# A hybrid encoder layer on one core: the projection's weights loaded at once into the filters' memory, and Hyena's projection begun at the last quarter of the sequence

## The chip, the cores and the metric

The kernel runs on one core of one Trainium2 chip. The metric is the time of one execution on the device in microseconds (us), the median of several runs. The core's engines are named as the profile names them: PE multiplies matrices (PEld loads the stationary operand for it), DVE, ACT and POOL work on vectors, SP issues most of the DMAs. Each engine takes its instructions in the order in which the program has them and waits at each one until what it needs is there. A "granted clock" of 1.00 in the profile is PE's full clock.

## The reference

One layer over 2048 tokens of width 1024, all float32. Cut to what the change touches:

```python
a = rms_norm(h, norm1_g)
proj = a @ w_in                               # (2048, 1024) @ (1024, 2304)
q, k, v, u = split(proj, [512, 640, 768])     # attention's columns, then Hyena's 1536
...                                           # per-head norm and rotary positions of q and k
att = block_attention(q, k, v)                # 8 query heads, 2 key heads of 64
uc = short_conv(u, conv_w, conv_b)            # three taps along the sequence, then the long filters
z = concatenate([t, cos(ang), -sin(ang)])     # the filters' own small network
h = sin(freq * (z @ w1 + b1)); h = sin(freq * (h @ w2 + b2)); h = sin(freq * (h @ w3 + b3))
...                                           # filters applied by Fourier transforms, output projection, MLP
```

## The kernel before

Matrix products of float32 are made of three products of rounded parts: each operand is split into a high part and the rest (`mm3`, lines 168 to 170: high by high, high by rest, rest by high). The norm's gain goes into the weights: ACT writes `wh` = weight times gain, rounded, and DVE writes `wl`, the rest (`split_w`, lines 214 and 215).

The program runs in stages. The first is `qkv_proj` together with pieces of two other generators, which it advances a step at a time with `pump`: `side` is `filter_hidden`, the hidden layers of the long filters, and `u` is `u_proj`, Hyena's projection and short convolution. In this stage the order of instructions on PE, DVE, ACT and POOL is the order of the code (`in_order`); SP's order is chosen by the scheduler. The second stage is `attention`, in which the scheduler mixes the rest of `u_proj` and the filters' taps into the attention steps. After it come the Fourier transforms of the filters and of Hyena's convolutions, the output projection and the MLP, which the change doesn't touch.

`qkv_proj` goes over 16 tiles of 128 tokens, in a pipeline that a loop over `i` writes out by hand. A tile of x is loaded (`xt`), squared and scaled by its norm (`xs`, lines 225 and 231), transposed on PE (`tp`, line 240), split into the high part `ah` (ACT, line 243) and the rest `al` (DVE, line 249), and multiplied with the weights: 8 by 3 matmuls of 512 columns for q and as many of 256 columns for k and v (`qkv`). Then ACT takes the result (`y`, `z`, line 272 on), DVE norms and rotates it (`rotation`), PE transposes it again (`tq`, line 316), and it is stored to DRAM (`q_d`, `k_d`, `v_d`). Both parts of every transposed tile are stored too, in `aT_d`, for `u_proj`.

The weights come in 16 pieces, eight of 128x512 for q and eight of 128x256 for k and v (`wraw`, line 210), into three buffers of the one and four of the other. SP issues a load when its buffer is free, that is when ACT and DVE have split the piece before it.

`filter_hidden` has its own memory (`f1`). Its first step, at `i` = 1, issues 16 small DMAs from POOL's queue and has DVE scale the loaded `fr` (line 1329); each of the next two steps issues a load of `z` (line 1345, POOL's queue again) and right behind it the matmuls `fo` that read it (line 1339). Later steps are matmuls, three DVE instructions each, sines on ACT, and copies into `hc`.

`u_proj` multiplies in 4 blocks of 512 tokens, from the first to the last, with 12 column tiles each, so 48 units of 8 times three matmuls (`uo`). A block's operand is loaded back from `aT_d` in eight pieces (`aT`, line 423). In the first block each unit's weights are loaded raw (`uraw`, line 434), split by ACT and DVE (`uw`, lines 438 and 440) and stored in `uw_d`, from where the other blocks load them; weights and raw weights have two buffers each, and the load for unit n+1 is issued when unit n begins. The result is copied (`u`), convolved by one ACT and two DVE instructions (`uy`) and stored. Within a block a unit is 10 steps of the generator. Before attention 38 steps of units are taken (the last 30 by `START`): not quite four units.

Of the kernel before, what the change touches and what calls it, by code (L numbers as in the profile page):

```python
# [172 lines left out]
def small_tables(k):  # L173
# [9 lines left out]
    nc.vector.tensor_scalar_mul(out=k.qkg[:, 0], in0=k.qkg[:, 0], scalar1=HD ** -0.5)  # L183


def qkv_proj(k, pa, ps, side, u):

    nc, a = k.nc, k.a
    x, w_in = a["x"][0], a["w_in"][0]
    root = pa.tile([P, 1], F32, name="root", bufs=1)  # L190
# [15 lines left out]
    raws = {}  # L206

    def load_w(d, c0, c1):
        raws[d, c0] = pw.tile([P, c1 - c0], F32, name=f"wraw{c0}", bufs=4 if c0 else 3)
        nc.sync.dma_start(out=raws[d, c0][:], in_=w_in[d * P:(d + 1) * P, c0:c1])  # L210

    def split_w(d, c0, c1):
        raw = raws.pop((d, c0))
        nc.scalar.mul(out=wh[:, d, c0:c1], in_=raw[:], mul=k.g1[:, d:d + 1])
        nc.vector.scalar_tensor_tensor(out=wl[:, d, c0:c1], in0=raw[:], scalar=k.g1[:, d:d + 1],
                                       in1=f32(wh[:, d, c0:c1]), op0=ALU.mult, op1=ALU.subtract)

    def load_x(t):
        xt[t] = pw.tile([P, DM], F32, name="xt", bufs=3)
        nc.sync.dma_start(out=xt[t][:], in_=x[t * P:(t + 1) * P, :])  # L220

    def squared(t):
        xs[t] = pa.tile([P, DM], F32, name="xs", bufs=3)
        ssq = pa.tile([P, 1], F32, name="ssq")
        nc.scalar.activation(out=xs[t][:], in_=xt[t][:], func=AF.Square, accum_out=ssq[:])
        rs[t] = []
        return rstd_steps(k, pa, ssq[:], DM, 1, "rstd", rs[t])

    def scaled(t):
        r, = rs.pop(t)  # L230
        nc.scalar.mul(out=xs[t][:], in_=xt.pop(t)[:], mul=r[:])
# [14 lines left out]
    def turned_low(t):  # L246
# [3 lines left out]
        for i, part in enumerate((hi, lo)):  # L250
            nc.sync.dma_start(out=k.aT_d[i, :, t * P:(t + 1) * P].rearrange("(d p) t -> p d t", p=P), in_=f32(part[:]))
# [79 lines left out]
    for d in range(4):  # L331
        load_w(d, *q_cols)
    load_x(1)
    for d in range(4, ND):
        load_w(d, *q_cols)
    for d in range(4):
        load_w(d, *kv_cols)
    load_x(2)
    for d in range(4, ND):
        load_w(d, *kv_cols)  # L340
    nc.gpsimd.dma_start(out=qkg[:, 0], in_=a["q_norm_g"].to_broadcast([P, HD]))
    nc.gpsimd.dma_start(out=qkg[:, 1], in_=a["k_norm_g"].to_broadcast([P, HD]))
    k.qkg = qkg
    small_tables(k)
    ahead = {-2: range(4), -1: range(4, ND)}
    for i in range(-3, NT + 2):
        norms = rot = iter(())
        own, mine = 0 <= i < NT, 0 <= i - 2 < NT
        tail = i >= NT
        if 2 < i + 5 < NT:  # L350
            load_x(i + 5)
# [4 lines left out]
        if tail:  # L356
            pump(u, 2)
# [9 lines left out]
        if 0 <= i + 2 < NT:  # L367
            scaled(i + 2)
        if i == -2:
            turned(0)  # L370
            turned_low(0)
        for d in ahead.get(i, ()):
            split_w(d, *q_cols)
        pump(rot)
        if 0 <= i + 3 < NT:
# [6 lines left out]
        if tail:  # L382
            pump(u, 2)
# [3 lines left out]
        if 0 < i + 1 < NT:  # L387
            turned(i + 1)
        pump(rot)
        if 0 < i + 1 < NT:  # L390
            turned_low(i + 1)
        if i == 0:
            for d in range(ND):
                split_w(d, *kv_cols)
# [9 lines left out]
        if i > 0:  # L404
            pump(side)
        pump(u, {NT - 5: 1, NT - 4: 3, NT - 3: 3, NT - 2: 3}.get(i, 0))
        if i == NT - 1:
            pw_pool.__exit__(None, None, None)
            pump(u)
# [4 lines left out]
def u_proj(k):  # L414
    nc, a = k.nc, k.a
    w_in = a["w_in"][0]
    nct = 3 * HYW // P
    H, NB = 512, 4
    cw, cb = k.cw, k.cb

    def load_a(b, d):
        t = pu.tile([P, 2, H], F32R, name="aT", bufs=ND)
        nc.sync.dma_start(out=f32(t[:]), in_=k.aT_d[:, d * P:(d + 1) * P, b * H:(b + 1) * H].rearrange("a p t -> p a t"))
        return t

    def load_w(b, ct):

        w = uws[(b * nct + ct) % 2]
        if b:
            nc.sync.dma_start(out=f32(w[:]), in_=k.uw_d[ct])  # L430
            return w, iter(())
        c0 = 768 + ct * P
        raw = raws[ct % 2]
        nc.sync.dma_start(out=raw[:], in_=w_in[:, c0:c0 + P].rearrange("(d p) c -> p d c", p=P))

        def split():
            for d in range(ND):
                nc.scalar.mul(out=w[:, 0, d], in_=raw[:, d], mul=k.g1[:, d:d + 1])  # L438
                if d in UW_VEC:
                    nc.vector.scalar_tensor_tensor(out=w[:, 1, d], in0=raw[:, d], scalar=k.g1[:, d:d + 1],  # L440
                                                   in1=f32(w[:, 0, d]), op0=ALU.mult, op1=ALU.subtract)
                else:
                    nc.gpsimd.tensor_mul(out=raw[:, d], in0=raw[:, d], in1=k.g1[:, d:d + 1].to_broadcast([P, P]))
                    nc.gpsimd.tensor_sub(out=w[:, 1, d], in0=raw[:, d], in1=f32(w[:, 0, d]))
                yield
            nc.sync.dma_start(out=k.uw_d[ct], in_=f32(w[:]))
            yield

        return w, split()

    uws, raws = [k.uf.tile([P, 2, ND, P], F32R, name="uw0")], [k.uf.tile([P, ND, P], F32, name="uraw0")]
    nw, rest = load_w(0, 0)
    yield
    for _ in rest:
# [3 lines left out]
    aT = [load_a(0, d) for d in range(ND)]  # L458
    uws.append(pu.tile([P, 2, ND, P], F32R, name="uw1", bufs=1))
# [1451 lines left out]
```

## Time and profile before

| | |
|---|---|
| median of 3 runs | 3138.62 us (3138.4 to 3143.3) |
| profiled execution | 3142.1 us, of which the span of instructions is 3140.3 us |
| mean granted clock of PE | 0.977 |
| PE busy | 2976.8 us, 95% of the span |
| DVE, ACT, POOL busy | 1984.8, 1394.4, 1713.8 us |
| moved by DMA | 534.16 MB, 170 GB/s over the span |

The profile is one execution, about 3.5 us above the median. A row of a timeline has the start, the duration, engine, line and operation, output and inputs, and in brackets the idle time of that engine just before and what ended it. A row of windows has the busy time and the count of instructions of each engine in a stretch, then the granted clock, the busy share of the DMA engines and GB/s. A row of a group has the count, then busy time and the mean of one in ns, then the idle time before them and its causes.

### The profile page before, as it was taken

Reading aid. Unit: us, or ns where it says so; the run is one execution under the profiler, and the core shown is the slowest. Engines: PE = TensorE matmul, PEld = TensorE weight load, DVE = VectorE, ACT = ScalarE, POOL = GpSimd, SP = SyncE. Lnnn points to the kernel's source line nnn. Section 1 sums busy time; section 2 is a strip of 40 time slices with the busy share of each in tenths; the row PEclk is TensorE's granted clock in tenths of the full one; section 3 lists DMA queues with packets and bytes.
Section 4 is the critical chain, followed back from the end, with each engine's and each line's share of the span. In section 5 each row is a group of like instructions: output and inputs, shape, how many; then the busy total and the mean of one; then the engine's idle time right before and its main releaser. Section 6 shows DMA issues by size and latency. Waiting matters only on the chain.

```text
span 3140.3 us, 40401 instructions
## 1 busy us (share of the span) xinstructions
PE 2976.8 (95%) x13384; PEld 2245.9 (72%) x13384; DVE 1984.8 (63%) x3050; ACT 1394.4 (44%) x2593; POOL 1713.8 (55%) x1424
## 2 busy tenths in 40 slices
PE   5896999999999998999999979999999999999998
PEld 4784666666666665676666767888788778888887
DVE  3675876656666664777465567777977544454455
ACT  4564665555555444444444553333433233223333
POOL 3230678787878888244555327767876643250010
PEclk8898999999999999999999989999999999999999
DMA  6669434325335324776656884445544393333454
GB/s 166 196 197 284 152 122 150 111 98 170 106 107 152 117 96 106 258 252 218 187 177 196 257 301 156 160 152 190 195 152 156 124 358 129 133 115 128 148 180 154
DMA packets 472304, 534.16 MB, mean 170 GB/s; under 512 B 39482, under 2 KB 334000, under 8 KB 465056
## 3 DMA queue, kind: packets, MB, share of 16 engines
q1 hardware_dynamic: 452624, 510.83, 50.0%
q0 software_dynamic: 5408, 15.18, 1.5%
q10 hardware_dynamic: 14064, 5.58, 0.7%
q8 instruction: 107, 1.75, 0.2%
q14 instruction: 101, 0.83, 0.1%
HBM read 325.95 MB, written 198.19 MB: 167 GB/s over the span
## 4 chain that ended last, share of the span: by engine, by line
PE 77%; DMA 4%; DVE 4%; issue 3%; POOL 2%; ACT 2%; SPq 0%; POOLq 0%; ACTq 0%; DVEq 0%
PE o L589 7%; PE y L169 6%; PE y L168 6%; PE y L170 6%; PE g L170 5%; PE g L169 5%; PE g L168 5%; PE st L568 4%; PE X L1536 4%; PE st L569 4%; PE sc L548 3%; PE uo L168 3%; PE uo L169 3%; PE uo L170 3%; PE b L1667 2%
## 5 line engine op out<-in xcount | busy, mean ns | idle before, releaser
L576 POOL TENSOR_TENSOR sum<-sum,p 128x512 f32<-128x512 f32 x416 | 555.7, 1336 | 98.2 <-ACT p L571 72.3
L551 DVE TENSOR_REDUCE top<-sc 128x1 f32<-128x512 f32 x512 | 348.5, 687 | 256.9 <-PE sc L548 253.3
L571 ACT ACTIVATE p<-st 128x512 f32<-128x512 f32 x512 | 302.7, 598 | 295.1 <-PE st L569 273.1
L168 PE MATMUL g<-mh,wop 128*128 128x512 f32 x896 | 351.4, 392 | 10.2 <-ACT wop L1008 8.2
L170 PE MATMUL g<-mh,wop 128*128 128x512 f32 x896 | 351.3, 392 | 1.9 <-DVE wop L1009 1.9
L169 PE MATMUL g<-ml,wop 128*128 128x512 f32 x896 | 351.4, 392 | 1.8 <-DVE ml L1019 1.8
L168 PE MATMUL y<-bh,ah 128*128 128x512 f32 x768 | 299.5, 390 | 12.4 <-ACT ah L1213 12.4
L169 PE MATMUL y<-bh,ah 128*128 128x512 f32 x768 | 299.4, 390 | 0.1
L170 PE MATMUL y<-bh,ah 128*128 128x512 f32 x768 | 299.3, 390 | 0.0
L1192 DVE TENSOR_TENSOR ah<-ar,ah 128x1024 fp32r<-128x1024 f32 x111 | 149.7, 1350 | 231.5 <-ACT ah L1191 231.5
L1191 ACT CAST ah<-ar 128x1024 fp32r<-128x1024 f32 x111 | 117.1, 1055 | 342.9 <-PE y L170 331.1
L589 PE MATMUL o<-p,vt 128*64 128x512 f32 x1024 | 237.3, 600 | 0.1
L568 PE MATMUL st<-q,kt 128*128 128x512 f32 x512 | 213.0, 416 | 1.4 <-ACT p L571 1.4
L548 PE MATMUL sc<-kt,q 128*128 128x512 f32 x512 | 202.0, 398 | 5.0 <-DVE top L551 4.5
L168 PEld LDWEIGHTS g<-mh,wop 128*128 128x128 f32 x896 | 169.9, 190 | 46.5 <-ACT wop L1008 8.9
L569 PE MATMUL st<-q,kt 128*128 128x512 f32 x512 | 200.5, 392 | 0.0
L170 PEld LDWEIGHTS g<-mh,wop 128*128 128x128 f32 x896 | 169.7, 189 | 38.5 <-DVE wop L1009 3.1
L169 PEld LDWEIGHTS g<-ml,wop 128*128 128x128 f32 x896 | 169.7, 189 | 37.5 <-DVE ml L1019 2.1
L1008 ACT CAST wop<-ws 128x512 fp32r<-128x512 f32 x128 | 79.3, 621 | 229.4 <-PE g L170 180.4
L168 PEld LDWEIGHTS y<-bh,ah 128*128 128x128 f32 x768 | 144.6, 188 | 42.9 <-ACT ah L1213 12.9
L168 PE MATMUL uo<-aT,uw 128*128 128x512 f32 x384 | 154.0, 401 | 19.7 <-ACT uw L438 9.6
L170 PEld LDWEIGHTS y<-bh,ah 128*128 128x128 f32 x768 | 144.4, 188 | 30.5 <-DVE ah L1214 0.3
(314 smaller groups left out, 6923.5 us busy)
## 6 DMA issues: line engine op xcount, KB each, us to landing
ar<-H_d SPq DMA_DIRECT2D x109, 512.0 KB, 3.7
uw<-uw_d SPq DMA_DIRECT2D x36, 1024.0 KB, 4.9
w1raw<-in_w_mlp_in SPq DMA_DIRECT2D x64, 512.0 KB, 4.1
H_d<-r SPq DMA_DIRECT2D x96, 256.0 KB, 2.2
H_d<-s SPq DMA_DIRECT2D x96, 256.0 KB, 2.0
F_d<-F SPq DMA_DIRECT2D x34, 512.0 KB, 3.2
F<-F_d SPq DMA_DIRECT2D x34, 512.0 KB, 3.7
aT<-aT_d SPq DMA_DIRECT2D x32, 512.0 KB, 6.0
```

The source lines that it names most:

```text
L168: mm(out, l_hi, r_hi, start=start, stop=False)
L169: mm(out, l_hi, r_lo, start=False, stop=False)
L170: return mm(out, l_lo, r_hi, start=False, stop=stop)
L548: nc.tensor.matmul(s[:], u.q[:, h], kt[u.kv, b][0][:], start=True, stop=True)
L551: k.mark_v = nc.vector.tensor_reduce(out=u.top[:, h, b:b + 1], in_=s[:], axis=AX.X, op=ALU.max, negate=True)
L568: nc.tensor.matmul(s[:], lo[:, c], u.q2[:].rearrange("p h t -> p (h t)"), start=True, stop=False)
L569: nc.tensor.matmul(s[:], hi[:, c], u.q[:].rearrange("p h t -> p (h t)"), start=False, stop=True)
L571: nc.scalar.activation(out=p[:], in_=s[:], func=AF.Exp)
L576: k.mark = nc.gpsimd.tensor_add(out=u.sum[:], in0=u.p0[:] if j == 1 else u.sum[:], in1=p[:])
L589: nc.tensor.matmul(u.o[cols], vt[j // 8][:, j % 8, u.kv], p[:], start=j < 2, stop=j > 13)
L1192: nc.vector.tensor_sub(out=h[:, 1], in0=raw[:], in1=f32(h[:, 0]))
L1536: k.nc.tensor.matmul(d[:, ri], t[:, m], Af[:, 2 * j + at], start=True, stop=True)
```

## The change

The first stage is rearranged in five ways.

1. `filter_hidden` works in one block of memory, `box` (16 rows of 512 numbers per partition). Its DMAs, the two loads of `z` among them, are its first step, which is now taken right after the first load of x; DVE's scaling of `fr` is at the head of the second step. From `i` = 8 on two of its steps are taken in each turn.
2. The 16 raw pieces of the weights have places of their own in `box` (rows 0 to 7 and 12 to 15), so their loads wait for nothing. x gets a ring of four tiles.
3. The order at the start is written anew: the splits of the q weights lie between the steps of the first two tiles, and the k and v weights are split in turn 0. DVE's scaling of the loaded `q_norm_g` moves from the very start into turn 0.
4. `u_proj` takes the blocks from the last to the first. The last four tiles of `qkv_proj` are split straight into its operand `A` (which takes `box`'s memory when the filters are done), so neither is the last quarter stored in `aT_d` nor loaded back; the other three quarters still are. The column that neighbouring blocks share is kept at the other end.
5. Raw weights of `u_proj` are loaded two units ahead, its first two units' weights are split inside the loop over tiles (in turns 7 to 9 and 14 to 15), and five whole units are done before attention, 16 steps of them in turn 16, 6 in turn 17 and 28 by `START`.

The numbers of matmuls, of splits and of other vector instructions stay the same, but for some copies and fills of single columns.

```diff
@@ qkv_proj @@
+    def raw_w(d, c0):
+        n = d if c0 == 0 else ND + d // 2
+        s = k.box[:, n if n < 8 else n + 4]
+        return s if c0 == 0 else s[:, d % 2 * 256:d % 2 * 256 + W - c0]
...
+    ring = k.uf.tile([P, 4, DM], F32, name="xt", tag="X")
...
     def turned(t):
-        hi = pa.tile([P, ND, P], F32R, name="ah", bufs=2)
-        lo = pa.tile([P, ND, P], F32R, name="al", bufs=2)
+        if t < NT - QT:
+            hi, lo = (pa.tile([P, ND, P], F32R, name=n, bufs=2)[:] for n in ("ah", "al"))
+        else:
+            if t == NT - QT:
+                k.A = k.uf.tile([P, ND, 2, QT * P], F32R, name="A", tag="A")
+            c0 = (t - NT + QT) * P
+            hi, lo = (k.A[:, :, i, c0:c0 + P] for i in range(2))
...
     load_x(0)
+    pump(side)
+    for d in range(ND):
+        load_w(d, *q_cols)
+    load_x(1)
+    for d in range(ND):
+        load_w(d, *kv_cols)
+    load_x(2)
+    load_x(3)
...
+    pump(squared(0), 3)
+    for d in range(2):
+        split_w(d, *q_cols)
+    scaled(0)
+    for d in range(2, 4):
+        split_w(d, *q_cols)
+    turned(0)
+    for d in range(4, 6):
+        split_w(d, *q_cols)
+    turned_low(0)
+    pump(squared(1), 3)
+    for d in range(6, ND):
+        split_w(d, *q_cols)
+    scaled(1)
+    pump(squared(2), 3)
...
-            pump(side)
-        pump(u, {NT - 5: 1, NT - 4: 3, NT - 3: 3, NT - 2: 3}.get(i, 0))
+            pump(side, 1 if i < 8 else 2)
+        pump(u, {NT - 10: 1, NT - 9: 3, NT - 8: 3, NT - 7: 4, NT - 3: 1, NT - 2: 4, NT - 1: 5, NT: 10}.get(i, 0))
@@ u_proj @@
+    for n in range(NB * nct):
+        b, ct = NB - 1 - n // nct, n % nct
+        w = uws[n and 2 - n % 2]
+        if n == 1:
+            ring = k.uf.tile([P, 2, ND, P], F32, name="uraw", tag="U")
+        if 0 < n < nct - 2:
+            raws[n + 2] = load_raw(n + 2, ring[:, n % 2])
+        parts = iter(())
+        if 0 < n < nct - 1:
+            parts = split(n + 1, raws[n + 1])
+        elif nct <= n + 1 < NB * nct:
+            nc.sync.dma_start(out=f32(uws[1 + n % 2]), in_=k.uw_d[(n + 1) % nct])
...
+            mm3(k, o[:], w[:, 0, d], w[:, 1, d], k.A[:, d, 0], k.A[:, d, 1], d == 0, d == ND - 1)
+            if ct == nct - 1 and b:
+                load_a(b - 1, d)
+            pump(parts)
@@ filter_hidden @@
+    box = k.box = k.uf.tile([P, 16, 512], F32, name="box", tag="A")
...
+    for b in range(2):
+        nc.gpsimd.dma_start(out=zs[b], in_=a["zT"][:, b * 512:(b + 1) * 512])
...
-START = 30
+START = 28
```

How the instructions move is seen best at three places. The first is ACT's program at the start. Before, from the scaling of tile 1 (`L231`) on, where `L225` is the square of a tile of x, `L120` a square root of its norm, `L243` the cast of a transposed high part and `L214` a split of weights:

```order
L231 ACTIVATE xs<-xt,rstd 128x1024
L214 ACTIVATE wh<-wraw_136,g_113 128x512
L214 ACTIVATE wh<-wraw_138,g_113 128x512
L214 ACTIVATE wh<-wraw_140,g_113 128x512
L214 ACTIVATE wh<-wraw_142,g_113 128x512
L225 ACTIVATE xs,ssq<-xt 128x1024
L120 ACTIVATE rstde<-rstdy 128x1
L231 ACTIVATE xs<-xt,rstd 128x1024
L225 ACTIVATE xs,ssq<-xt 128x1024
L120 ACTIVATE rstde<-rstdy 128x1
L243 CAST ah<-tp 128x512 x2
L214 ACTIVATE wh<-wraw_144,g_113 128x256
```

The same place of ACT in the changed kernel, from the last two q splits and the scaling of tile 1 on (the lines are now 218 for splits, 231, 237 and 256):

```order
L218 ACTIVATE wh<-box,g_110 128x512 x2
L237 ACTIVATE xs<-xt,rstd 128x1024
L231 ACTIVATE xs,ssq<-xt 128x1024
L120 ACTIVATE rstde<-rstdy 128x1
L218 ACTIVATE wh<-box,g_110 128x256 x8
L237 ACTIVATE xs<-xt,rstd 128x1024
L231 ACTIVATE xs,ssq<-xt 128x1024
L120 ACTIVATE rstde<-rstdy 128x1
L256 CAST ah<-tp 128x512 x2
```

The last `L256` row and the `L243` row are the cast of tile 1. The eight splits for k and v, which followed that cast, now stand ahead of it, behind the square of tile 2.

The second place is POOL's queue of DMAs. Before, in turn 1 of the loop, between POOL's work on tiles 0 and 1 (`kk`, `y`):

```order
L274 TENSOR_TENSOR y<-y,qkg 128x512
L1319 MEMSET w_471 66x128
L1319 MEMSET w_472 128x128
L1319 MEMSET w_473 128x256
L1322 DMA w_471<-in_filt_w 33x64
L1323 DMA w_472<-in_filt_w 64x64
L1325 DMA w_473<-in_filt_w 64x64 x2
L1327 DMA fb<-in_filt_b 64x1 x3
L1328 DMA fr<-in_filt_freq 64x1
```

After, at the very start of POOL's program, behind the fills of constants:

```order
L198 MEMSET unit 128x1
L1332 DMA box<-in_zT 66x512 x2
L1333 MEMSET box 128x512
L1336 DMA box<-in_filt_w 33x64
L1337 DMA box<-in_filt_w 64x64
L1340 DMA box<-in_filt_w 64x64 x2
L1342 DMA box<-in_filt_b 64x1 x3
L1343 DMA box<-in_filt_freq 64x1
```

All of the filters' DMAs, `z` first, now stand ahead of POOL's first vector work.

The third place is SP's queue at the end of the first stage. Before, with `L423` the operand of `u_proj`, `L434` its raw weights and `L326`/`L278` the stores of tiles 14 and 15:

```order
L326 DMA k_d<-qs 128x4x128
L423 DMA aT<-aT_d 128x2x512 x8
L434 DMA uraw_2582<-in_w_in 128x8x128
L278 DMA v_d<-v 128x128
L326 DMA q_d<-qs 128x4x128 x2
```

After, where `L457` stores split weights and `L446` loads raw ones:

```order
L457 DMA uw_d<-uw_2251 128x2048
L291 DMA v_d<-v 128x128
L339 DMA q_d<-qs 128x4x128 x2
L339 DMA k_d<-qs 128x4x128
L446 DMA uraw<-in_w_in 128x8x128 x2
L516 DMA u_d<-uy 128x511
```

The eight loads of `aT` are gone there, and two raw weights are loaded behind one another where one was.

More of the change, by code (lines that the diff above doesn't have):

```diff
@@ L417, in u_proj @@
     nct = 3 * HYW // P
-    H, NB = 512, 4
+    H, NB = QT * P, NT // QT
     cw, cb = k.cw, k.cb
+    uws = [k.uf.tile([P, 2, ND, P], F32R, name="uw0", tag="U")[:]]
     def load_a(b, d):
[L422 to L446, printed above, removed]
```

220 lines of the change are left out of this document (102 added, 118 removed).

## The prediction

> **What bounds the kernel now.** I read the windows by stage first. The rows are: the weights and the first tile; the rest of the loop over tiles; the end of the first stage, which is the start of Hyena's projection; the start of attention; the rest of attention; all that follows.
>
> ```profile
> 0.00:47.00 47.00, 21.34 (x64) 14.79 (x65) 15.09 (x43) 21.64 (x39) 7.75 (x15) 0.81 0.75 195
> 47.00:241.50 194.50, 169.18 (x1018) 143.97 (x1016) 128.49 (x289) 114.92 (x246) 73.80 (x113) 0.93 0.65 189
> 241.50:296.50 55.00, 32.45 (x121) 24.44 (x121) 24.04 (x69) 22.81 (x59) 5.23 (x9) 0.75 0.90 275
> 296.50:350.00 53.50, 45.11 (x160) 27.30 (x161) 49.97 (x93) 37.74 (x82) 20.56 (x16) 0.97 0.68 206
> 350.00:1220.00 870.00, 868.43 (x3854) 575.67 (x3853) 550.89 (x868) 471.43 (x862) 701.54 (x530) 1.00 0.37 120
> 1220.00:3140.00 1920.00, 1840.27 (x8173) 1459.71 (x8171) 1216.36 (x1689) 725.88 (x1308) 904.94 (x743) 0.98 0.56 186
> ```
>
> From 350 to 1220 us PE is busy for 868 of 870 us at full clock: attention is bound by PE, and work that leaves it or comes to it shortens or lengthens it by its own PE time. Before 296.5 us PE idles for 25.7, 25.3 and 22.6 us in three stretches and runs below full clock, so a wait removed there should come off the end. From 296.5 to 350 us it is DVE that is full (49.97 of 53.5). The list of PE's waits up to 296.5 us says for whom PE waits; the columns are the total, the times and the longest.
>
> ```profile
> PE fo L1339 <- DMA z<-in_zT: 17.7, 2, 14.0
> PE qkv L168 <- ACT wh L214: 13.7, 6, 5.5
> PE tp L240 <- ACT xs L231: 11.2, 1, 11.2
> PE uo L168 <- ACT uw L438: 9.6, 2, 8.1
> PE uo L168 <- DMA aT<-aT_d: 9.5, 3, 7.3
> PE tq L316 <- ACT ah L243: 4.4, 4, 1.5
> ```
>
> The change goes at the first five of these rows. I therefore sum three terms of gain, by stretch, and one of loss.
>
> **The start (term A).** Below are three rows of the start, the rate of the DMAs while PE waits for its first data, and the groups of which ACT's chain is made.
>
> ```profile
> 8.56 0.20 DVE L183 TENSOR_SCALAR qkg<-qkg 128x64 f32<-128x64 f32 x1 [6.94 <-DMA qkg<-in_q_norm_g]
> ...
> 23.72 0.72 ACT L214 ACTIVATE wh<-wraw,g 128x512 fp32r<-128x512 f32 x1 [8.09 <-DMA wraw<-in_w_in]
> ...
> 47.09 0.63 PE L168 MATMUL qkv<-wh,ah 128*128 128x512 f32 x1
> ```
>
> ```profile
> 3.00:10.00 7.00, 0.00 (x0) 0.00 (x0) 0.90 (x6) 1.42 (x4) 4.66 (x4) 1.00 1.00 246
> ```
>
> ```profile
> L231 ACT ACTIVATE xs<-xt,rstd 128x1024 f32<-128x1024 f32 x16 | 18.7, 1167 | 2.6 <-DVE rstd L125 2.6
> ...
> L243 ACT CAST ah<-tp 128x512 fp32r<-128x512 f32 x32 | 17.3, 594 | 2.4 <-PE tp L240 2.4
> L225 ACT ACTIVATE xs<-xt 128x1024 f32<-128x1024 f32 x16 | 16.7, 1044 | 2.4 <-DMA xt<-in_x 2.4
> ...
> L214 ACT ACTIVATE wh<-wraw,g 128x256 fp32r<-128x256 f32 x8 | 3.5, 503 | 3.0 <-DMA wraw<-in_w_in 3.0
> ```
>
> Tile 1's q matmuls begin at 47.09 us. Two waits made them late: DVE stood behind `q_norm_g` until 8.56 us with tile 0's norm queued behind it, and the weights came in turns through few buffers (ACT 8.09 us idle for the fourth piece). Both go. What is late next is the row of loads itself. In the new ACT order the cast of tile 1, which those matmuls need, stands behind the square of tile 2, and tile 2 is loaded behind all weights: three tiles of x at 0.52 MB, 2.1 and 1.05 MB of weights and 0.27 MB of `z` make 5.0 MB. At 246 GB/s, with the first bytes after about 2 us, that is there at 22 us; at the 195 GB/s of the whole stretch, at 28 us. From there ACT does a square (1.04), eight splits (8 x 0.50), a scaling (1.17), a square (1.04) and two casts (2 x 0.59), 8.5 us, and about 1 us of small steps: matmuls at 31.5 to 37 us. I take 32, nearer to the rate of a row in which only such loads run, so **A = 15 us**, with 10 and 17 as ends (17 if ACT's splits overlap as closely as before). PE's own work up to there is short enough to lie in front of it. The filters' small DMAs and tables go out on POOL's queue meanwhile; their first readers come at `i` = 1.
>
> **The loop (term B).** PE's two waits for `z`, how they came about, and the clock behind them:
>
> ```profile
> 69.57 0.15 DVE L1329 TENSOR_SCALAR fr<-fr 128x1 f32<-128x1 f32 x1 [13.09 <-DMA fr<-in_filt_freq]
> ...
> 77.78 0.57 POOL L1345 DMA_DIRECT2D z<-in_zT  x1
> ...
> 82.18 2.04 PE L1339 MATMUL fo<-z,w 66*128 66x512 f32 x2 [13.96 <-DMA z<-in_zT]
> ...
> 99.78 1.10 PE L1339 MATMUL fo<-z,w 66*128 66x512 f32 x2 [3.76 <-DMA z<-in_zT]
> ```
>
> ```profile
> 80.00:90.00 10.00, 7.82 (x24) 5.65 (x25) 5.53 (x14) 3.09 (x6) 0.43 (x1) 0.63 0.50 150
> 100.00:105.00 5.00, 5.00 (x17) 3.61 (x17) 3.93 (x9) 2.75 (x5) 0.00 (x0) 0.66 0.36 93
> 158.60:192.00 33.40, 33.40 (x217) 29.00 (x216) 24.31 (x54) 24.70 (x51) 12.51 (x18) 1.00 0.83 240
> ```
>
> DVE waits 13.09 us for `fr`, POOL behind DVE, the load of `z` behind POOL, and PE, which has nothing else in its order, behind `z`. With these DMAs issued at the start all four waits go: 13.96 + 3.76 = 17.7 us. Behind each wait PE ran at a lower granted clock: 7.82 busy us at 0.63 lose up to 2.9, 5.00 at 0.66 up to 1.7. That is up to 22.3 us; **B = 22**, with 19 (a clock that is low there for other reasons) and 23 as ends. Nothing else is late just behind: three turns without a wait (158.6 to 192) are 11.1 us of pure PE each, with DVE and ACT at 24 and 25 of 33.4 us.
>
> The Trainium skill ("TensorE: Matmul & The Clock Gate", section on the HAM clock gate) says that PE falls to half clock after an idle window of about 3.4 us and needs about as long a busy one to come back. The rows above agree: 0.63 and 0.66 right behind waits of 14 and 3.8 us. By that rule the two gaps of some 3 us that I expect at the new start could each cool the clock once more, and the sum would be up to 3.4 us smaller.
>
> The filters' later steps and the first split of `uw` move from turns 12 to 14 into turns 7 to 10, two filter steps a turn. The cover is the 8 us per turn and engine that the last row leaves idle for three turns. If it doesn't hold it costs a few us, as PE's waits for `ah` (4.4) do in turns 11 to 14 now; these go in return, so I set it to 0, with 4 on either side.
>
> **The end of the first stage (term C).** The rows are SP's issue of the eight loads of `aT`, the first and the last wait of PE for them, ACT's wait for the filters' last weights, and the wait of PE behind it.
>
> ```profile
> 244.12 7.95 SPq L423 DMA_DIRECT2D aT<-aT_d  x8
> ...
> 250.54 0.79 PE L168 MATMUL uo<-aT,uw 128*128 128x512 f32 x1 [7.33 <-DMA aT<-aT_d]
> ...
> 262.42 0.50 PE L168 MATMUL uo<-aT,uw 128*128 128x512 f32 x1 [1.25 <-DMA aT<-aT_d]
> ...
> 287.90 0.62 ACT L1381 CAST w4h<-w 128x512 fp32r<-128x512 f32 x1 [5.90 <-DMA w<-in_filt_w]
> ...
> 288.88 0.79 PE L168 MATMUL uo<-aT,uw 128*128 128x512 f32 x1 [8.05 <-ACT uw L438]
> ```
>
> One step of a warm run of `uo` matmuls, from the chain of waits, then DVE's group for the filters' last weights, and the fastest 5 us of the stretch's DMAs:
>
> ```profile
> 273.10 0.23 PE uo L170
> ```
>
> ```profile
> L1382 DVE TENSOR_TENSOR w4l<-w,w4h 128x512 fp32r<-128x512 f32 x4 | 2.8, 692 | 9.1 <-ACT w4h L1381 9.1
> ```
>
> ```profile
> 255.00:260.00 5.00, 5.00 (x23) 4.00 (x23) 0.00 (x0) 1.18 (x2) 0.00 (x0) 0.69 1.07 398
> ```
>
> Between 241.5 and 296.5 us PE does 32 groups of three `uo` matmuls. After the change it does 40, from an operand that is already in memory and with weights split ahead. Warm, a group is 3 x 0.23 = 0.69 us: 27.6 us, and 24 transposes of the last tiles some 2.8, together 30.4 us if nothing else is late. The 8 groups more (5.5 us) come out of attention, which PE bounds. So the gain is 55.0 + 5.5 - T, with T the new stretch. What could be late next is DMA: the stretch moved 55 us x 275 GB/s = 15.1 MB. Without `aT` (4.2 MB) and with half a MB more of results, 11.4 MB remain, which at 275 GB/s take 41.5 us. Not all of it gates PE, since stores of `uw_d` and results are only waited for two units later; I take T = 37, so **C = 23**, with 41.5 (19) and 30.4 (30) as ends.
>
> The Trainium skill ("DMA: Bandwidth & Descriptors", Specifications) gives about 358 GB/s as the limit of one core at the memory; as an estimate by it, T would be at least 11.4 MB / 358 = 32 us and C at most 28.5. The row with 398 GB/s differs, so the measurement decides: at that rate the bytes take 28.6 us, less than PE's 30.4, and the upper end stays.
>
> **The start of attention (term D).** The weights of the filters' last layer (`w4`) were prepared inside the stretch above; in the new order two of their four casts and all four DVE instructions (2.8 us) stand behind its end, where DVE is full, and the later two wait for a DMA as the one with 5.90 us did. On the other side DVE has one tile of `uw` less to split there. I take **D = -3**, with -8 (the whole wait and the 2.8) and +2 as ends.
>
> **The sum.** 15 + 22 + 23 - 3 = 57 us. Against the profiled execution's 3142.1 us that is 3085; the runs' median stands 3.5 us below it, so 3138.6 - 57 gives **3081.6 us**.
>
> **The rivals.** First, DMA becomes the bound: everything asked for earlier queues up, and the end of the stage is no shorter than its 55 us. For it speaks the DMA share of 0.90 there, against it that 4.2 of 15.1 MB go. C is then only the 5.5 us: 15 + 22 + 5.5 - 3 = 39.5, 3099 us. Second, at the start the change doesn't do what it says: loads still come one behind another, tile 2 stands behind 5 MB, and ACT behind tile 2. If the small tables of 4-byte elements slow the loads as far as 43 us for tile 1, A is 4, and the time 3092.6. Third, the gain is given back: attention is paced by something other than PE, and its 870 us grow by what it starts earlier. The row with 868 us of PE speaks against it; 3138.
>
> On the other side: `A` is one tile where `aT` was eight. If a new block's loads wait for the whole of the old block instead of for their own eighth, PE, in order, stands at each of the three switches inside attention from the issue to the last landing: 262.42 - 244.12 = 18.3 us as in the rows above, 2.9 us of lower clock as behind the longer wait in the loop, and 4.3 us for the next unit's 1.05 MB of weights behind them at 246 GB/s, 25.5 us. Three times that less 57 is 19.5 us lost, 3158 us. It decides from 19 us a switch. Against it: before, the same loads showed no wait there, and in the new order each eighth waits for its own matmuls.
>
> **How the numbers follow.** My forecast has 0.77, the first rival 0.10, the second 0.06, the third 0.03, the slower one 0.04. The ends of the terms give gains of 10 + 19 + 19 - 8 = 40 and 17 + 23 + 30 + 2 = 72, or 3098 and 3066 us; I stretch the range to 3064 and 3104, which takes in the first two rivals. A measurement of this kernel can tell about 0.2%, 6 us, from no change. Faster by more: 0.77 + 0.10 + 0.06 = 0.93; same 0.03; slower 0.04.
>
> **What would show it.** In the new profile: tile 1's q matmuls at 31 to 37 us; no wait of `fo` for a DMA; granted clock 1.00 from about 50 us on but for the sines; no `uo` wait for `A` before attention, the first `sc` of attention near 240 us; after it DVE full for some 50 us; then PE at 99% as before. I am wrong if the first stage's end is not 50 to 60 us earlier, or if it is and attention ends less than that earlier.

## The result and the profile after

The changed kernel takes **3089.0 us** (median of its runs) where the kernel before, on the same chip, takes 3139.2: the ratio is 0.9838, with an interval of 0.982 to 0.9855. That is 50 us, against 57 forecast. The profiled execution took 3092.75 us, with a span of 3091.0, 49.3 less than the span before.

The windows of the changed kernel, cut to within half a microsecond at the same events as those of before: tile 1's q matmuls, the end of the loop's q, k and v matmuls, the first `sc`, 53.5 us later, the end of attention.

```profile
0.00:26.50 26.50, 13.95 (x64) 11.32 (x64) 13.21 (x40) 19.86 (x37) 16.94 (x33) 1.00 0.94 264
26.50:201.60 175.10, 163.74 (x1021) 140.95 (x1021) 136.49 (x299) 119.47 (x261) 68.14 (x96) 0.99 0.71 206
201.60:230.90 29.30, 29.30 (x143) 24.19 (x142) 21.61 (x65) 17.81 (x47) 3.06 (x6) 1.00 0.88 285
230.90:284.40 53.50, 42.94 (x140) 25.42 (x138) 47.61 (x98) 37.81 (x85) 15.32 (x12) 0.84 0.76 248
284.40:1166.00 881.60, 877.91 (x3850) 575.77 (x3851) 552.02 (x864) 471.13 (x858) 706.31 (x535) 1.00 0.35 117
1166.00:3090.00 1924.00, 1842.45 (x8173) 1461.08 (x8171) 1220.96 (x1689) 725.43 (x1308) 905.50 (x743) 0.98 0.57 186
```

The three stretches ahead of attention went from 47, 194.5 and 55 us to 26.5, 175.1 and 29.3, and PE is full in the third. The first `sc` comes at 230.87 us in place of 296.02, 65.1 us earlier; the kernel ends only 49.3 earlier. So the changed stretches gave more than forecast, and 16 us were lost behind them. The list of PE's waits up to 230.8 us (total, times, longest) has none for a DMA any more; its three longest rows are

```profile
PE tp L253 <- ACT xs L237: 10.1, 1, 10.1
PE fo L1356 <- ACT box L1349: 4.6, 2, 2.4
PE tq L329 <- ACT ah L256: 4.0, 2, 2.5
```

Four rows of the new start and of the new end of the first stage: ACT takes up tile 2 of x, tile 1's q matmuls begin, the first `uo` and the first `sc` run.

```profile
18.73 1.06 ACT L231 ACTIVATE xs<-xt 128x1024 f32<-128x1024 f32 x1 [0.20 <-DMA xt<-in_x]
...
26.54 0.50 PE L168 MATMUL qkv<-wh,ah 128*128 128x512 f32 x1
...
201.60 0.47 PE L168 MATMUL uo<-A,uw 128*128 128x512 f32 x1
...
230.87 0.39 PE L563 MATMUL sc<-kt,q 128*128 128x512 f32 x1
```

Behind the first `sc` the profile looks worse than before. ACT waits for the filters' last weights, DVE behind ACT, PE behind DVE; the window below them has the DMAs full and PE at half clock.

```profile
241.57 0.62 ACT L1397 CAST w4h<-w 128x512 fp32r<-128x512 f32 x1 [3.67 <-DMA w<-in_filt_w]
...
242.22 0.69 DVE L1398 TENSOR_TENSOR w4l<-w,w4h 128x512 fp32r<-128x512 f32 x1 [3.21 <-ACT w4h L1397]
...
243.57 1.39 PE L563 MATMUL sc<-kt,q 128*128 128x512 f32 x2 [3.72 <-DVE top L566]
```

```profile
235.00:250.00 15.00, 9.50 (x17) 4.31 (x16) 10.81 (x19) 7.57 (x16) 0.00 (x0) 0.50 1.06 342
```

To see where attention lost time, I cut it at the 41st `sc` matmul, at 357.1 us before and 298.1 after. First the two windows of before, then the two of after:

```profile
296.00:357.10 61.10, 52.62 (x186) 30.30 (x185) 55.74 (x106) 42.04 (x90) 21.84 (x17) 0.94 0.65 201
357.10:1220.20 863.10, 861.53 (x3830) 572.86 (x3829) 545.38 (x856) 467.40 (x854) 700.47 (x529) 1.00 0.37 119
```

```profile
230.90:298.10 67.20, 54.96 (x186) 33.03 (x185) 59.33 (x117) 45.47 (x100) 22.95 (x17) 0.85 0.72 235
298.10:1166.10 868.00, 865.99 (x3806) 568.24 (x3805) 540.30 (x844) 463.47 (x844) 698.78 (x529) 1.00 0.35 116
```

The start is 6.1 us longer. The long rest is 4.9 us longer although 24 projection matmuls (8 groups of three) have left it. PE is full in both and hardly waits; the whole list of its waits from 298 to 1166 us after the change is

```profile
PE of L615 <- POOL ob L609: 0.9, 1, 0.9
PE st L583 <- ACT p L586: 0.4, 2, 0.2
PE sh L576 <- DVE top L566: 0.3, 1, 0.3
```

A full PE that takes longer for less work does each piece of it more slowly. The groups of attention say so. One group of scores and one of the projection, before (358 to 1220 us) and after (298 to 1166 us); the last two numbers ahead of the idle time are busy us and mean ns of one:

```profile
L548 PE MATMUL sc<-kt,q 128*128 128x512 f32 x471 | 183.2, 391 | 0.0
...
L169 PE MATMUL uo<-aT,uw 128*128 128x512 f32 x336 | 131.0, 390 | 0.0
```

```profile
L563 PE MATMUL sc<-kt,q 128*128 128x512 f32 x472 | 185.5, 395 | 0.1
...
L169 PE MATMUL uo<-A,uw 128*128 128x512 f32 x328 | 129.3, 394 | 0.0
```

Each takes about 1% more, at a granted clock of 1.00 in both. If all of PE's work in some 860 us slowed like that, it would be 7 to 8 us; not all does (the `o` matmuls take 599 ns in both). None of it was in the sum.

### The profile page after: what moved, and what is told of

It reads as the page before. It is cut to its first block, busy times and chain, and to the rows that moved or that the text cites. A ratio compares the mean times of both kernels' runs of the same rounds, so it can differ in the third digit from the quotient of the medians.

```text
span 3091.0 us, 40376 instructions
## 1 busy us (share of the span) xinstructions
PE 2970.3 (96%) x13384; PEld 2238.7 (72%) x13384; DVE 1991.9 (64%) x3050; ACT 1391.5 (45%) x2593; POOL 1715.3 (55%) x1422
## 4 chain that ended last, share of the span: by engine, by line
PE 79%; DVE 4%; DMA 3%; issue 3%; POOL 3%; ACT 2%; SPq 0%; ACTq 0%; POOLq 0%; DVEq 0%
PE o L604 7%; PE y L168 7%; PE y L170 7%; PE y L169 7%; PE g L169 5%; PE g L170 5%; PE g L168 5%; PE st L583 4%; PE X L1552 4%; PE st L584 4%; PE sc L563 4%; PE uo L169 3%; PE uo L170 3%; PE uo L168 3%; PE b L1683 2%
## 5 line engine op out<-in xcount | busy, mean ns | idle before, releaser
L168 PEld LDWEIGHTS g<-mh,wop 128*128 128x128 f32 x896 | 169.2, 189 | 45.0 <-ACT wop L1023 9.7
L168 PEld LDWEIGHTS y<-bh,ah 128*128 128x128 f32 x768 | 144.8, 189 | 43.1 <-ACT ah L1228 13.0
L170 PEld LDWEIGHTS y<-bh,ah 128*128 128x128 f32 x768 | 144.8, 189 | 30.7 <-DVE ah L1229 0.3
L169 PEld LDWEIGHTS y<-bh,ah 128*128 128x128 f32 x768 | 144.8, 189 | 30.0
```

Source lines behind the costliest of these rows:

```text
L168: mm(out, l_hi, r_hi, start=start, stop=False)
L169: mm(out, l_hi, r_lo, start=False, stop=False)
L170: return mm(out, l_lo, r_hi, start=False, stop=stop)
```

## The experiments

Medians are set against 3089.0 for the changed kernel; the ratios are to the kernel before, timed beside each. "First `sc`" and "last `st`" are the begin of attention's first and last score matmul in the profile, 230.9 and 1166.1 us after the change. The "pace" is the mean of the `sc` and `uo` rows of attention with a single matmul of 512 columns that lie between 0.38 and 0.43 us (some 1500 a profile; rows at a lowered clock fall out). PE begins a matmul before the one ahead of it is through, so the pace is not the time from one to the next: `uo` matmuls that follow one another in attention begin on average 0.2284 us apart before the change and 0.2313 after. The intervals of the ratios are some 4 us wide to either side; where two medians lie nearer than that, the traces have to carry the argument.

**The pace: the same kernel again, and one line that moves memory.** The diff also takes out `aligned(pu, 160)`, which holds 160 bytes of each partition empty behind the tile `edge`. Attention's pool starts behind that one, so by the addresses in the built programs its large tiles slid from multiples of 256 bytes to 96 past one (the score keys from 126464 to 126304). The forecast had no term for that line. The first run changes nothing, the second puts the line back, the third takes it out of the kernel before:

```
@@ e5_gap_back, in the changed kernel
     edge = pu.tile([P, nct, 2], F32, name="edge", bufs=1)
+    aligned(pu, 160)
@@ e6_before_no_gap, in the kernel before
     edge = pu.tile([P, nct, 2], F32, name="edge", bufs=1)
-    aligned(pu, 160)
```

> The changed kernel once more, nothing edited. Its four runs fell in two pairs, 3085.5 and 3085.9, 3092.1 and 3092.8 us, and in the profiled one of the slow pair a matmul of attention took 0.395 us where before it took 0.3915 (860 us of PE times 0.9% is 7.7 us). Theory 1: this pace is a matter of the execution, not of the change; then these runs spread again over 3085 to 3093, and a profiled execution near 3085 shows 0.391 to 0.392 in attention. Theory 2: the change slows the matmuls (more bytes moved beside them, other places in memory); then every profile of this kernel shows 0.394 to 0.396 there, and the two pairs have another cause.

> The changed kernel with one line more, the gap of 160 bytes that the change left out behind the tile edge: attention's tiles then start where they did before the change (the score keys at byte 126464 of each partition and not 126304, so at a multiple of 256 and not 96 past one). Five profiles of kernels with the change all show 0.3947 us for a matmul of attention, the one before 0.3915. Theory 1: these places in memory set the pace; then a matmul takes 0.391 to 0.392 us again, attention is some 7 us shorter, and the time about 3082. Theory 2: the pace goes with the new projection (its operand, its weights, its order); then it stays at 0.3947 and the time at 3089.

> The kernel before with that one line taken out, nothing else of the change. Theory 1 (the places set the pace): a matmul of attention takes 0.3947 us and the time is 6 to 9 us longer than before, some 3147. Theory 2 (the new projection sets it): 0.3915 us and no difference.

The same kernel again: 3089.05 us, pace 0.3947 in a profile of 3090.0 us, so the pace goes with the kernel and not with the execution. With the line back: pace 0.3915, last `st` at 1158.9 us, 3083.6 us (ratio 0.9818, 0.9805 to 0.9832). The kernel before without the line: pace 0.3947, the stretch from the 41st `sc` to the last `st` 869.9 us in place of 863.1, 3145.4 us (1.0015, 1.0005 to 1.0025). The `uo` matmuls begin 0.2285 us apart with the line back, and 0.2313 in the kernel before without it. Theory 1 holds from both sides. The same groups with the line back, then of the kernel before without it:

```profile
L564 PE MATMUL sc<-kt,q 128*128 128x512 f32 x472 | 183.8, 391 | 0.2
...
L169 PE MATMUL uo<-A,uw 128*128 128x512 f32 x328 | 127.9, 390 | 0.0
```

```profile
L547 PE MATMUL sc<-kt,q 128*128 128x512 f32 x471 | 185.0, 395 | 0.4 <-DVE ao L603 0.4
...
L169 PE MATMUL uo<-aT,uw 128*128 128x512 f32 x336 | 132.4, 394 | 0.0
```

Two looks at other distances, with gaps of 32 and of 96 bytes in the changed kernel:

> The changed kernel with a gap of 32 bytes, so that attention's tiles start at 128 past a multiple of 256. If a multiple of 64 or of 128 is enough, a matmul of attention takes 0.3915 us as with the gap of 160; if it must be 256, 0.3947 as without a gap, or between.

> The changed kernel with a gap of 96 bytes, so that attention's tiles start at 192 past a multiple of 256, at a multiple of 64 and not of 128. If a multiple of 64 is enough, 0.3915 us a matmul; if it must be 128 or 256, 0.3947 or between.

At 128 past a multiple of 256 the pace is 0.3941, at 192 past 0.3933. So of the four places tried only the multiple of 256 has the fast pace; the other two lie between. In time they gained nothing: from the 41st `sc` to the last `st` they took 868.5 and 867.2 us, against 868.0 at 96 past and 862.2 with the line back, and their single executions took 3090.4 and 3097.3 us. In the first stage, whose own tiles stand 128 past a multiple, the pace from 60 to 150 us is 0.3944 before and 0.3943 after; the last experiment moves these too.

**Term B: the filters' DMAs back in turn 1.** The second side step of each turn begins one turn earlier, so that the filters still end in time.

```
-    for b in range(2):
-        nc.gpsimd.dma_start(out=zs[b], in_=a["zT"][:, b * 512:(b + 1) * 512])
+    yield
     nc.gpsimd.memset(box[:, 10], 0.0)
...
-    yield
     nc.vector.tensor_scalar_mul(out=fr, in0=fr, scalar1=1.0 / (2.0 * math.pi))
+    yield
...
     for b in range(2):
+        nc.gpsimd.dma_start(out=zs[b], in_=a["zT"][:, b * 512:(b + 1) * 512])
         args.append(argument(w1, zs[b], fb[:, 0:1]))
```

> The changed kernel, but with the filters' DMAs back in turn 1, fr scaled behind them and each load of z behind that, as before the change. Theory (term B: the waits for z came off the end one for one): PE waits again some 14 and 4 us for z, and with the clock behind them the time is 15 to 22 us longer than the changed kernel's, about 3104 to 3110. Rival: the first stage's end is set by its DMAs or by DVE, so that a wait in its middle is made up by the end; then 0 to 6 us longer.

3114.9 us (0.9922, 0.9908 to 0.9935), 25.9 more, above the 15 to 22 expected; the first `sc` comes at 256.6 us, 25.7 later than the changed kernel's. The two waits are back at almost their old lengths, and the two windows with them show the granted clock:

```profile
66.22 2.05 PE L1355 MATMUL fo<-box 66*128 66x512 f32 x2 [13.45 <-DMA box<-in_zT]
...
84.88 2.05 PE L1355 MATMUL fo<-box 66*128 66x512 f32 x2 [3.99 <-DMA box<-in_zT]
```

```profile
60.00:70.00 10.00, 3.78 (x10) 2.38 (x11) 2.47 (x5) 3.17 (x9) 4.12 (x6) 0.50 0.63 177
85.00:90.00 5.00, 5.00 (x13) 3.28 (x14) 2.93 (x6) 1.69 (x3) 0.00 (x0) 0.50 0.18 53
```

17.4 us of waits and some 8 us behind them: PE's 8.78 busy us at 0.50 in these two windows lose 4.4, and what the others are I did not part. The rival is out: nothing later makes up for a wait there. The Trainium skill ("TensorE: Matmul & The Clock Gate", Part 1 on the HAM clock gate) has PE at half clock behind an idle window of about 3.4 us; the trace agrees, for the wait of 3.99 us too.

**Term A: loads that wait for slots.** Two tries. The first only let pieces share slots:

```
-        n = d if c0 == 0 else ND + d // 2
+        n = d % 4 if c0 == 0 else ND + d % 4 // 2
```

> The changed kernel, but the raw weights of the first stage share four slots of 512 columns and four of 256, so that a load waits for the split of the piece before it in its slot, as before the change. The norm's scaling stays where the change put it. Theory (term A came from the loads, all at once): SP stands at the fifth weight, tiles 1 and 2 of x are loaded behind it, and tile 1's q matmuls begin 6 to 12 us later than at 26.5 us; the time grows by as much, to 3095 to 3101. Rival: DVE's wait for the norm's vector was what made the start late; then the matmuls begin within 2 us of 26.5 and the time grows by under 3 us.

3089.6 us, no difference, and no answer. The loads stand ahead of the splits in the program, so a later load waits only for the load before it in its slot, not for a split; the first four pieces of q, and of k and v, are split from the later pieces' numbers. The second try asks for each of the later pieces behind the split that frees its slot:

```
     for d in range(2):
         split_w(d, *q_cols)
+        load_w(d + 4, *q_cols)
...
             for d in range(ND):
                 split_w(d, *kv_cols)
+                if d < 4:
+                    load_w(d + 4, *kv_cols)
```

> The changed kernel, but each of the last four raw weights of q, and of k and v, is loaded into the slot of one before it and asked for behind that one's split, so that it must wait for it, as before the change. Theory (term A came from the loads, all at once): SP stands at the fifth weight, tiles 1 and 2 of x are loaded behind it, tile 1's q matmuls begin 4 to 10 us later than at 26.5 to 27 us, and the time grows by as much. Rival: the norm's vector, for which DVE stood, made the start late, and four slots are enough; then the matmuls begin within 2 us of that and the time grows by under 3 us.

3098.7 us (0.9864, 0.9849 to 0.9879), 9.7 more. ACT's wait for k and v's fifth piece, and the begin of tile 1's q matmuls:

```profile
29.80 1.71 ACT L218 ACTIVATE wh<-box,g 128x256 fp32r<-128x256 f32 x4 [6.96 <-DMA box<-in_w_in]
...
34.54 0.79 PE L168 MATMUL qkv<-wh,ah 128*128 128x512 f32 x1 [0.94 <-ACT ah L256]
```

The size is the theory's, 8 us at the start; the place is not. x was hardly later (ACT takes up tile 2 at 19.66 us in place of 18.73). It was the last four pieces of k and v that came late, and behind their splits in ACT's row the cast of tile 1. The rest of term A's 20.5 us must lie in what this kernel keeps: the norm's scaling off the front, a fourth place for the pieces of q, and the new order of ACT's and SP's work. I did not part these.

**Term C: the last quarter through main memory.** Tiles 12 to 15 get the small tiles `ah` and `al` and are stored like the others; `A` is loaded as the projection begins.

```
-        if t < NT - QT:
+        if True:
             hi, lo = (pa.tile([P, ND, P], F32R, name=n, bufs=2)[:] for n in ("ah", "al"))
...
+    k.A = k.uf.tile([P, ND, 2, QT * P], F32R, name="A", tag="A")
+    for d in range(ND):
+        load_a(NB - 1, d)
     for n in range(NB * nct):
```

> The changed kernel, but the last quarter's operands go through the chip's main memory like the others: tiles 12 to 15 are stored, and loaded into A when the projection begins. Theory (term C came from the operand in place): PE waits for A at the end of the first stage, 8 to 15 us, and 8.4 MB more pass in a stretch whose DMAs were full from 210 us on; the first score matmul comes 10 to 25 us later than at 230.9 us, and the time grows by as much, to 3098 to 3113. Rival: C came from the weights split earlier and from the steps' new places; then under 5 us longer.

3099.5 us (0.9872, 0.9859 to 0.9886), 10.5 more; first `sc` 12.3 later. PE waits four times for `A`, 7.1 us together:

```profile
214.79 0.80 PE L168 MATMUL uo<-A,uw 128*128 128x512 f32 x1 [4.04 <-DMA A<-aT_d]
...
243.14 0.39 PE L565 MATMUL sc<-kt,q 128*128 128x512 f32 x1
```

So the operand in place is worth some 10 to 12 of term C's 25 us, at the low end of what I expected, and the waits a little below it. Where the others come from no run here shows. Two things are gone in this kernel too and may be it: before, PE waited 9.6 us for weights that were not yet split, and its 32.45 busy us of that stretch had a granted clock of 0.75 (0.91 here).

**Term D: the filters' last weights from GpSimd's queue.** The fourth of the weights borrows the first of the tiles `ex`, which is not used yet.

```
-        w4 = f1.tile([P, HYW], F32, name="w4", tag="taps", bufs=3)
+        w4 = f1.tile([P, HYW], F32, name="w4", **(dict(tag="taps", bufs=3) if c < 3 else dict(tag="ex", bufs=2)))
         for i in range(2):
-            nc.scalar.dma_start(out=w4[i * FH:(i + 1) * FH], in_=a["filt_w4"][0, :, c * HYW:(c + 1) * HYW])
+            nc.gpsimd.dma_start(out=w4[i * FH:(i + 1) * FH], in_=a["filt_w4"][0, :, c * HYW:(c + 1) * HYW])
```

> The changed kernel, but the eight loads of the filters' last weights are issued on GpSimd's queue, which is empty there, and not in ACT's row of work, and the fourth weight has a place of its own from the start. Theory (term D: attention starts slowly since DVE stands for these loads, and PE behind DVE): no wait of ACT for them, PE's waits for DVE between the first score matmul and 245 us shrink from some 8 us to under 3, and the time is 3 to 6 us shorter, 3083 to 3086. Rival: DVE is full behind that wait anyway, or the loads push out others from DMA queues that are full from 210 to 250 us; then no more than 1.5 us.

3081.4 us (0.9811, 0.9796 to 0.9827), 7.6 less; last `st` at 1158.6, 7.5 earlier. The loads go out from 213.18 us, in one row; before this edit the last of them went out at 237.4 us, in between ACT's other work. PE's waits for DVE shrink to one of 1.3 and one of 1.0 us. One wait of 4.04 us for ACT is new, and it did not undo the gain. A load took no less time from its issue to its landing (7.7 us in the median, 7.2 without the edit), so what helped is that they are asked for earlier, and not a faster queue; the queue and the fourth weight's place were changed together, and which of them allows it was not tried. With the edit the scheduler also put some of attention's first PE instructions in another order; how much of the 7.6 us, more than I expected, is due to that, these runs don't say.

```profile
213.18 4.20 POOL L1396 DMA_DIRECT2D w<-in_filt_w  x8 [3.74 <-issue]
...
234.18 1.22 PE L563 MATMUL sc<-kt,q 128*128 128x512 f32 x2 [4.04 <-ACT u L502]
```

**The 5.5 us that left attention.** The windows behind the last `uo` of before, then of after, and GpSimd's sums of that stretch after the change:

```profile
1200.30:1220.20 19.90, 19.75 (x77) 8.48 (x76) 3.48 (x4) 10.02 (x18) 17.88 (x15) 1.00 0.18 60
```

```profile
1130.20:1166.10 35.90, 34.89 (x131) 15.70 (x130) 7.55 (x14) 17.20 (x31) 33.81 (x26) 1.00 0.12 37
```

```profile
L591 POOL TENSOR_TENSOR sum<-sum,p 128x512 f32<-128x512 f32 x22 | 29.5, 1341 | 2.0 <-ACT p L586 0.4
```

GpSimd is busy for 33.81 of 35.9 us there, at one sum of 1.34 us for two `st` (0.665 us each, in both kernels). PE reads as full in either window, but without the `uo` matmuls it gets through no more `st`. With eight groups done ahead, the projection ends earlier, and this part of attention grows from 19.9 to 35.9 us.

```
-RATE = 1.0
+RATE = 0.96
```

> The changed kernel with 0.96 steps of side work for one step of attention in place of 1.0, so that the projection's last matmuls come some twelve steps later. The eight groups that left attention (5.5 us of PE) did not make it shorter: from the last projection matmul to the last of attention's st matmuls there are 54 of these, 35.9 us, where before there were 30, 19.9 us, 0.665 us each in both. Theory: there GpSimd's sums (1.336 us for two st) set the pace, and the 5.5 us went into PE's slack; spread over all steps, they come off the end: under 20 st behind the last projection matmul and 3 to 6 us less, 3083 to 3086. Rival: PE is the bound all along, and the order within attention doesn't matter; then 3087 to 3091.

3086.5 us (0.9829, 0.9815 to 0.9842). Ten `st` matmuls stand behind the last `uo` in place of 54, and from first `sc` to last `st` it is 931.5 us, 3.7 less than in the changed kernel's first profile and 3.4 less than in its second (935.2 and 934.9). The medians differ by 2.5 us, less than a measurement can tell. The traces carry it: six profiles of kernels with the changed kernel's attention and pace (its own two and those of the two experiments on term A, of term B and of term C) took 933.8 to 935.6 us for that stretch, and this one lies below them all. So PE had slack at attention's end, and the gain is at the low end of what was expected. That it is GpSimd's sums that PE goes by there rests on GpSimd's full row; no run made the sums faster.

**All together.** The gap, the weights' queue, the side steps, and `aligned(pa, 96)` made `aligned(pa, 224)`, which moves the first stage's own tiles to multiples of 256.

> The changed kernel with the gap of 160 bytes back, the filters' last weights loaded from GpSimd's queue, 0.96 side steps a step, and the first stage's own tiles moved from 128 past a multiple of 256 bytes to a multiple. If the gains add up: 5.5 for the gap, 7.6 for the weights, 3 to 6 for the steps, together 16 to 19, 3070 to 3073. If they overlap (the weights' gain came from a later end of the side work, as the steps' would): 3074 to 3078. If the first stage's places count as attention's do, its matmuls take 0.391 us and not 0.3945 between 50 and 150 us, worth 1 to 2 us; if only an odd multiple of 32 bytes counts, they stay at 0.3945.

**3073.3 us**, 0.9786 of the kernel before (0.9772 to 0.9799), 15.7 less than the changed kernel. The single gains (5.4, 7.6, 2.5) come to 15.5: they add up, as far as medians that are uncertain by some 4 us can tell, and this version beats both. Last `st` at 1149.8. In attention the pace is 0.3916, and in the first stage, from 60 to 150 us, 0.3909 in place of 0.3943: the places count there as well. In time that is not seen: the loop's last q, k and v matmul ends at 202.1 us, against 201.5 in the changed kernel.

## Why the prediction was right, and where it was not

The direction, the range and three of the mechanisms were right; the sum was 7 us too good, through errors that partly paid for each other. That it came so near is in part luck. Ahead of attention the change gave 10.6 us more than forecast (A 5.5 more, B 2.5 less, the first stage's end 7.6 more), attention gave 13.5 less, and 4.8 were lost behind it.

Both of the forecast's own signs of being wrong came out: the first stage's end is 65.1 us earlier and not 50 to 60, and attention ends only 54.1 us earlier. Of what it expected in the profile, four things came true: `fo` waits for no DMA, no `uo` waits for `A`, DVE is full behind the first `sc` (47.61 of 53.5 us), and PE is full after that. Three did not: tile 1's q matmuls at 31 to 37 us (26.54), the first `sc` near 240 us (230.87), and full clock from 50 us on (0.50 from 235 to 250 us).

The q and the k, v matmuls of the loop end at 241.48 us before and at 201.47 after; the last row runs from the last `st` to the end of the span.

| term | forecast | measured | by |
|---|---|---|---|
| A, the start | 15 (10 to 17) | 20.5 | 47.09 to 26.54 us |
| B, the loop | 22 (19 to 23) | 19.5 | 194.4 to 174.9 us |
| C, the first stage's end | 23 (19 to 30), 5.5 of it in attention | 25.1, and none in attention | 54.5 to 29.4 us |
| D, attention's start | -3 (-8 to 2) | -6.1 | 61.1 to 67.2 us |
| the rest of attention | 0 | -4.9 | 863.1 to 868.0 us |
| all behind attention | 0 | -4.8 | 1920.1 to 1924.9 us |
| sum | 57 | 49.3 | |

- **A: mechanism right, size too small and out of its bounds.** The step that failed is the landing of tile 2, "there at 22 us". It was there at 18.7: from 3 to 18.7 us the DMAs moved 327 GB/s and not 246.

```profile
3.00:18.70 15.70, 6.26 (x18) 4.66 (x19) 8.51 (x21) 11.05 (x18) 12.33 (x21) 1.00 0.98 327
```

  I had taken the rate of the old order of loads; from 3 to 10 us, where that one moved 246 GB/s, the new one moves 306. ACT's work from there took 7.8 us in place of 9.5; eight splits in a row are 3.29 us, not 8 x 0.50. The 1.00 in this row's clock is no reading: the trace's records of the clock begin at 19.5 us, and up to 19.4 us a q matmul of 512 columns takes 0.63 us, as in attention at a granted clock of 0.50, and 0.39 after that. PE works from 15.4 to 26.4 us without a wait, so its own work no longer lies "short enough" ahead of ACT's, as the forecast had it; the two rows end together.
- **B: right.** Both waits for `z` are gone, and undoing the hoist alone brings them back. PE's idle time in the stretch fell by 14.0 us (25.3 to 11.4) and not by 17.7, its busy time by 5.4 (169.2 to 163.7), where the forecast had up to 4.6 for the clock. What I gave nothing is the next wait in the row: PE waits 4.6 us for the sines (3.2 before) and 1.5 for the rotation.
- **C: the total about right, by two errors.** "T = 37" leaned on the DMAs as the bound. T was 29.4 us, just under what PE alone needs (30.4). The 11.4 MB were not all due in it: 29.3 us at 285 GB/s are 8.4 MB, and in the 53.5 us behind the first `sc` 2.2 MB more moved than before (248 GB/s in place of 206), beside the weights of term D. The other error is "the 8 groups more (5.5 us) come out of attention, which PE bounds". They came out, and attention was not shorter, since PE has slack at its end, where GpSimd's row is full; the run with 0.96 side steps gets some 3.5 us of it back.
- **D: right in sign and mechanism**, twice the size, and within its bounds: all four casts of the weights, and not two, stand behind the first `sc`, three of them wait for a DMA (5.5 us together), DVE for them, PE for DVE. Loads that go out earlier undo it (61.6 us from the first to the 41st `sc`). The forecast had no term for the clock: PE's 9.50 busy us at 0.50 could lose up to 4.7; in the run with the earlier loads the clock of the same 15 us is 0.73, and the runs don't part that loss from the waits.
- **Left out: the gap.** The line taken out explains all of the 4.9 us lost in the rest of attention: with it back the stretch is 862.2 us (296.7 to 1158.9), 0.9 less than before, with 5.5 us of projection less in it.
- **Behind attention** nothing was changed, and the 4.8 us are no effect of the change as far as these runs show: the same code took 1916.4 to 1927.0 us in the profiles of the twelve experiments, 1922.7 of the changed kernel's second profile.
- **The rivals.** DMA as the bound of the first stage's end: out, PE is full there. A start that doesn't do what it says: out. The gain given back in attention: it happened in part, 11 of 65 us, but not because attention is paced by something else throughout; it was late loads and one gap, while the 5.5 us taken out were not gained. The slower case, `A` as one tile: no wait for `A` stands among PE's waits in attention, which fits each eighth being released by its own matmuls.

## What to carry to other kernels

Sum a change by stretch, and ask of each stretch what ends it: a wait that ends a stretch alone comes off one for one, and PE work moved out of a full stretch is worth nothing once another engine's row is as long. Read each line of a diff that shifts memory, the empty gaps too, as a line that may cost: compare the mean time of the same matmul before and after, not only busy shares and waits. When loads are asked for earlier, look which later load they now meet, and give it a queue on which nothing stands ahead of it.

## What the runs showed of the hardware

- The time of PE's matmuls depends on where the tiles in use stand in a partition: 0.3915 us for 512 columns with attention's tiles at multiples of 256 bytes, 0.3933 at 192 past, 0.3941 at 128 past, 0.3947 at 96 past. From one `uo` matmul to the next it is 0.228 us at multiples of 256 and 0.231 at 96 past. The groups at 128 past, then at 192 past:

```profile
L564 PE MATMUL sc<-kt,q 128*128 128x512 f32 x470 | 184.5, 395 | 0.1
...
L169 PE MATMUL uo<-A,uw 128*128 128x512 f32 x327 | 128.5, 393 | 0.0
```

```profile
L564 PE MATMUL sc<-kt,q 128*128 128x512 f32 x471 | 184.4, 394 | 0.1
...
L169 PE MATMUL uo<-A,uw 128*128 128x512 f32 x327 | 128.7, 394 | 0.0
```

  The projection's matmuls slow down as well, though their own operands kept their places at multiples of 256. So it is not only PE's own reading of a shifted operand; whose reads or writes of the shifted tiles it is (ACT's, DVE's, GpSimd's or the DMAs') was not tried and stays open.
- The DMAs of this one core moved 342 GB/s over 15 us (235 to 250 us) and 327 over 15.7 us at the start.
